# Two blocks on one core: the stores of a normalised memory, two small loads, and the order of the blocks in a mixer

## The chip, the cores and the metric

The kernel runs on one NeuronCore of a Trainium2 chip. Its engines run beside each other, each through its own list of instructions in order, and wait for one another by semaphores: PE (TensorE, matrix products), DVE (VectorE), ACT (ScalarE), POOL (GpSimd) and SP, which here only issues DMA transfers. The metric is device time in microseconds (us), the median of several runs.

## The reference, cut to what matters

The inputs are 512 tokens of width 1024 and a memory of 256 rows. Two transformer blocks run one after the other, in float32:

```
mod = c @ w_ada + b_ada                          # shift, scale, gate
h   = rmsnorm(x) * (1 + scale) + shift
y_a = (stick_breaking(q_a, k_a, v_a) * silu(z_a)) @ w_o_sb        # q_a.. = h @ w_in
y_b = (forgetting_attention(q_b, k_b, v_b, cumsum log f) * silu(z_b)) @ w_o_fox
x   = rmsnorm(x + gate * ((g0 * y_a + g1 * y_b) @ w_out), final_g)
# second block
h1  = rmsnorm(x);  q, k, v, u = h1 @ w_in_2
a   = rmsnorm((softmax(q1 k1) - lam * softmax(q2 k2)) @ v)        # 4 heads, q and k rotated
c   = silu(layernorm(causal_dwconv(u[:512] * sigmoid(u[512:]), 31 taps)))
x   = x + concat(a, c) @ w_out_2
x   = x + cross_attention(rmsnorm(x), rmsnorm(mem)) @ w_co        # needs mem @ w_ckv
x   = x + conv_ffn(rmsnorm(x));  out = rmsnorm(x)
```

`lam` comes from four vectors of 64 numbers (one load of 128 KB, each vector repeated on all partitions); the rotation's angles come from the positions (one load of 2 KB).

## The kernel before, in words

Every large product is done in three passes, so that float32 accuracy is kept: each operand is split into a rounded half `h` and a remainder `l`, and `wh*xh + wh*xl + wl*xh` are summed in PSUM (`mm3`). A weight unit is 128 x 1024 floats (512 KB). `load` (L153) brings one into one of three `wr` buffers, `split` makes `wh` on ACT (L166) and `wl` on DVE or POOL (L167); which of the two is given by letters, D or P, in strings such as `START_LO` and `B2_LO`. A `wr` buffer is free again when its `wl` is made.

**The front** is written out by hand (`manual_schedule`): there PE, ACT, DVE, POOL and SP each keep the order in which the program text names their instructions. It loads the memory (two tiles `mr`, split into the eight tiles `mt`), x (four loads `xt`), sixteen units of `w_ada` (`ada_load`, tag `ar`, eight buffers) and ten units of `w_ckv`. A loop over n = 0 to 9 does in each round: two `ada_load` (rounds 0 to 5), `mem_split(n + 2)` which also issues the load of unit n + 5, the squares of two of the eight parts of x (`squares_x`, rounds 0 to 3: ACT squares, DVE adds into `xacc`, L463), the products of unit n on PE (`mem_unit`), a few idle products (`spin`), and two `ada` steps (L447, a multiply and sum on DVE, then a small ACT step), two per round from round 1 to 8. In round 4 PE sums `xacc` (L517), the inverse root goes through DVE and ACT (L265 to L270), and in round 5 it is broadcast into `xrb`. From round 6 on `token_h` makes two parts of h a round: y on DVE (L469), the rounded half on ACT (L471), the remainder on DVE (L473). Everything after the front needs all eight parts of h.

**After the front** the eight tiles `mt` are stored to DRAM (`ms_d`, L536, 256 KB each); the mixer reads them back for the value products of the memory. This store loop stands outside the hand-written order, as do the loads of `lam` (L727, into a tile of the pool `smp`) and of the positions (L740, also `smp`) that stand in the text behind the heads of the first attention. What stands outside is placed by a planner at compile time: it takes each instruction when its inputs and buffers are free by its own estimate of times. It may put such instructions between those of the front on the same engine, and it does: the trace shows these DMAs, and the DVE and ACT work on `lam` and on the angles (L730 to L769), inside the front. A tile of a pool that is opened after the front's pools are closed lies on their memory, and has to wait until that is released.

**The mixer** is again written by hand for PE, ACT, DVE and POOL (SP's order is the planner's). `BLOCKS` lists 34 weight units in order: `q2`, `k2`, `v2` are projections by halves (two units for two heads), `u2:c` and `u2:c+4` make chunk c of the convolution's input, `cd:c` does taps 0 to 7 of chunk c as products with diagonal matrices on PE, `mv` are the memory's values, `wo2a` the output projection of the attention half. `AFTER` says which head step or norm step follows which block: q, k (transposes and splits), s (scores of the first row block), t (the other rows), x (transposes of the probabilities), v (values), n and o (norm of the head's output); l0 to l4 are the layernorm of the convolution (mean, squares, variance, broadcast, output). When `cd:c` is done, 15 taps are put into a list for DVE (L1075, each adds into the PSUM bank of the chunk), 8 into a list for ACT and POOL (L1069, L1070), and a last step adds the two (`ca`, L1081). After each block up to 4 of the first list and 3 of the second are emitted. Before a new `cd`, `fill(99)` emits all that is left of DVE's list, since all four chunks use the one bank `sm`.

## Time and profile before

| what | value |
|---|---|
| median of 3 runs (range) | 1298.86 us (1298.73 to 1303.45) |
| the profiled execution: its time, its span | 1301.26 us, 1299.5 us |
| PE busy | 1228.8 us, 95% of the span |
| weight loads of PE, DVE, ACT, POOL busy | 1031.6, 772.6, 604.3, 454.4 us |
| granted TensorE clock, mean | 0.977 |
| DMA over the span | 140.09 MB, mean 108 GB/s |

The page was taken on the one core. Busy times are sums of the instructions' own durations; a granted clock of 1.00 is 2.4 GHz, and a stretch at 0.65 was partly at 1.2 GHz. A time in brackets behind an instruction is how long its engine stood idle before it, and the arrow names what ended that. In the windows view the columns are the stretch, its length, then each engine's busy time with its count of instructions, the granted clock, the DMA share and the rate.

### The profile page before, as it was taken

To read this page: it belongs to the slowest core of one execution; us is meant where nothing else is said; L and a number is where in the kernel's file an instruction comes from. 1 tells how busy PE (TensorE), PEld (TensorE's weight loads), DVE (VectorE), ACT (ScalarE), POOL (GpSimd) and SP (SyncE) were. 2 spreads that over 40 slices of the span, in tenths; PEclk is the share of its full clock that TensorE was granted. 3 is DMA by queue.
4 is the path that set the end of the run, shared out by engine and by line. 5 is a ranking of instruction groups with operands and counts; after the bars stand their busy time and mean duration, and the time that the engine had idled before them with its cause. 6 is when DMAs were issued, how large, how long until landed. Compare 5 with 4: busy or idle time off the path is not lost.

```text
span 1299.5 us, 16841 instructions
## 1 busy us (share of the span) xinstructions
PE 1228.8 (95%) x6376; PEld 1031.6 (79%) x6381; DVE 772.6 (59%) x1241; ACT 604.3 (47%) x993; POOL 454.4 (35%) x303
## 2 busy tenths in 40 slices
PE   6699999999999999998898888999999999999997
PEld 4678887988878888886887776887888888888886
DVE  3775768555475274457577758466587777771113
ACT  3554566455663345356365535444444444442222
POOL 1464444322222138334572527203422222222321
PEclk9899999999999999999899888999999999999998
DMA  9734222232148342231143324211333332222221
GB/s 358 267 131 138 81 74 73 66 91 83 63 150 293 107 130 88 77 90 41 57 128 108 90 98 130 81 50 50 112 97 98 98 97 98 97 90 89 89 89 65
DMA packets 46017, 140.09 MB, mean 108 GB/s; under 512 B 5233, under 2 KB 8817, under 8 KB 45938
## 3 DMA queue, kind: packets, MB, share of 16 engines
q1 hardware_dynamic: 45170, 136.93, 32.6%
q0 software_dynamic: 768, 2.10, 0.4%
q8 instruction: 50, 0.82, 0.2%
q14 instruction: 29, 0.24, 0.1%
HBM read 127.48 MB, written 8.39 MB: 105 GB/s over the span
## 4 chain that ended last, share of the span: by engine, by line
PE 79%; DVE 10%; ACT 4%; DMA 3%; issue 2%; POOL 1%; SPq 0%; DVEq 0%; ACTq 0%; POOLq 0%
PE lin L148 66%; PE z L148 7%; PE pv L148 3%; PE sm L148 2%; DMA wr<-in_wts 2%; DMA ar<-in_wts 1%; PE z L612 1%; DVE ar L447 1%; DVE sm L1075 1%; DVE wl L167 1%; ACT wh L166 1%; DMA xt<-in_x_t 1%; POOL wl L167 1%; POOL rb L1070 0%; DVE h L225 0%
## 5 line engine op out<-in xcount | busy, mean ns | idle before, releaser
L148 PE MATMUL lin<-h,wh 128*128 128x512 f32 (+1 forms) x2232 | 693.6, 391 | 10.5 <-ACT wh L166 6.6
L148 PEld LDWEIGHTS lin<-h,wh 128*128 128x128 f32 x2232 | 416.8, 191 | 97.4 <-ACT wh L166 9.7
L148 PE MATMUL lin<-h,wl 128*128 128x512 f32 (+1 forms) x1116 | 432.6, 388 | 7.8 <-POOL wl L167 6.9
L167 POOL TENSOR_TENSOR wl<-wr,wh 128x1024 fp32r<-128x1024 f32 (+1 forms) x116 | 281.1, 2424 | 435.3 <-ACT wh L166 399.9
L166 ACT CAST wh<-wr 128x1024 fp32r<-128x1024 f32 (+1 forms) x197 | 204.5, 1040 | 253.0 <-PE lin L148 164.7
L148 PEld LDWEIGHTS lin<-h,wl 128*128 128x128 f32 x1116 | 213.0, 191 | 49.7 <-POOL wl L167 8.3
L167 DVE TENSOR_TENSOR wl<-wr,wh 128x1024 fp32r<-128x1024 f32 (+1 forms) x81 | 106.6, 1316 | 123.0 <-ACT wh L166 122.5
L148 PE MATMUL lin<-wh,h 128*128 128x256 f32 x672 | 127.4, 286 | 2.3 <-DVE h L1010 2.3
L148 PEld LDWEIGHTS lin<-wh,h 128*128 128x128 f32 x672 | 106.8, 193 | 2.8 <-issue 2.4
L1382 DVE SCALAR_TENSOR_TENSOR cv<-up,vecs,cv 128x512 f32<-128x512 f32 x88 | 94.2, 1071 | 18.3 <-ACT cv L1380 16.8
L148 PE MATMUL lin<-wl,h 128*128 128x256 f32 x336 | 95.7, 285 | 0.4 <-POOL wl L167 0.4
L148 PE MATMUL lin<-zz,wh 128*128 128x512 f32 (+1 forms) x324 | 91.5, 368 | 0.0
L683 POOL TENSOR_TENSOR zs<-zs,y 64x512 f32<-64x512 f32 x16 | 26.6, 1665 | 120.3 <-DVE y L682 104.2
L148 PEld LDWEIGHTS lin<-zz,wh 128*128 128x128 f32 x324 | 58.0, 187 | 11.6
L148 PEld LDWEIGHTS lin<-wl,h 128*128 128x128 f32 x336 | 64.7, 193 | 0.8 <-POOL wl L167 0.7
L148 PE MATMUL lin<-zz,wl 128*128 128x512 f32 (+1 forms) x162 | 59.6, 368 | 0.0
L321 POOL TENSOR_TENSOR nacc<-nacc,sq 128x512 f32<-128x512 f32 x34 | 52.6, 1558 | 16.7 <-ACT sq L320 16.2
L1377 POOL MEMSET up<- 128x2 f32 x44 | 4.3, 99 | 148.4 <-DVE cv L1382 116.3
L1075 DVE SCALAR_TENSOR_TENSOR sm<-cp,vecs,sm 128x512 f32<-128x512 f32 x60 | 45.2, 754 | 1.6
L218 DVE TENSOR_TENSOR tl<-z,th 128x512 fp32r<-128x512 f32 (+1 forms) x60 | 33.4, 595 | 17.1 <-ACT th L217 16.7
L1389 ACT ACTIVATE cv<-cv 128x512 f32<-128x512 f32 x22 | 13.9, 632 | 59.6 <-DVE cv L1382 59.6
L612 PE MATMUL z<-idf,p 128*128 128x128 f32 x200 | 34.3, 282 | 7.5 <-ACT p L1172 2.6
(398 smaller groups left out, 1717.8 us busy)
## 6 DMA issues: line engine op xcount, KB each, us to landing
wr<-in_wts SPq DMA_DIRECT2D x197, 512.0 KB, 3.5
ar<-in_wts SPq DMA_DIRECT2D x16, 512.0 KB, 6.8
qk<-qk SPq DMA_DIRECT2D x24, 128.0 KB, 2.2
wr<-in_wts SPq DMA_DIRECT2D x8, 384.0 KB, 3.0
xt<-in_x_t SPq DMA_DIRECT2D x4, 512.0 KB, 8.8
ms_d<-h SPq DMA_DIRECT2D x8, 256.0 KB, 7.9
kv_d<-kvo POOLq DMA_DIRECT2D x16, 128.0 KB, 4.2
ma_d<-gt SPq DMA_DIRECT2D x8, 256.0 KB, 5.3
```

The lines of the kernel that those rows point to most:

```text
L148: pe.matmul(o, lhsT=lhsT, rhs=rhs, start=start, stop=stop, skip_group_check=True)
L166: act.copy(out=hi[:, :n], in_=raw[:, :n])
L167: lo_engine().tensor_tensor(out=lo[:, :n], in0=raw[:, :n], in1=f32(hi[:, :n]), op=ALU.subtract)
L218: dve.tensor_tensor(out=lo, in0=src, in1=f32(hi), op=ALU.subtract)
L321: pool.tensor_tensor(out=acc, in0=acc, in1=q, op=ALU.add)
L447: dve.scalar_tensor_tensor(out=r, in0=r, scalar=1.0, in1=cb, op0=ALU.mult, op1=ALU.mult, accum_out=m)
L612: pe.transpose(z[:, o + i * P:o + (i + 1) * P], pt[rb_][:, ro:ro + P], ident)
L683: pool.tensor_tensor(out=zs[r], in0=zs[r], in1=y[r], op=ALU.mult)
L1075: dve.scalar_tensor_tensor(out=cz, in0=x_, scalar=w_, in1=cz, op0=ALU.mult, op1=ALU.add)
L1377: pool.memset(up[:, T:], 0.0)
L1382: dve.scalar_tensor_tensor(out=r, in0=up[:, 2 - j:2 - j + T], scalar=V("ffn_w", c * 3 + j), in1=r, op0=ALU.mult, op1=ALU.add)
L1389: act.activation(out=a, in_=a, func=AF.Silu)
```

## The change

- The store loop of `mt` is indented into the front's hand-written part, behind `memory_squares()`: SP issues the eight stores after all other DMAs of the front.
- `squares_x` comes before `mem_split(n + 2)` in each round.
- The remainder of the third unit of `w_ckv` is made on DVE (`START_LO`).
- The tiles of `lam` and of the positions move from `smp` to the pool `gp`, which is opened after the front is closed.
- In the mixer the blocks are reordered: `cd:1` stands 5 blocks after `cd:0` (before: 3), `cd:2` 7 after that (before: 5), `cd:3` 3 after that (before: 5); `q2`, `k2` of heads 2 and 3 come before `cd:1`; two `mv` units each stand between `cd:2` and `cd:3`, behind `cd:3` and between the `wo2a` units. The steps follow, and with them the letters of `B2_LO` and the place of `memory_back`.
- `cd:3` uses the PSUM bank `pv` instead of `sm`, and no `fill(99)` stands before it.

```diff
-START_LO = "DDPPPPPPPP"
+START_LO = "DDDPPPPPPP"
...
-B2_LO = 24 * "P" + 5 * "DP"
+B2_LO = 23 * "P" + "DPPDPDPDPDP"
...
-BLOCKS = ("q2:0 q2:1 k2:0 k2:1 u2:0 u2:4 v2:0 v2:1 u2:1 u2:5 cd:0 u2:2 u2:6 cd:1 q2:2 q2:3 k2:2 k2:3 cd:2 u2:3 u2:7 "
-          "v2:2 v2:3 cd:3 mv:2 mv:3 mv:4 mv:5 mv:6 mv:7 wo2a:0 wo2a:1 wo2a:2 wo2a:3")
+BLOCKS = ("q2:0 q2:1 k2:0 k2:1 u2:0 u2:4 v2:0 v2:1 u2:1 u2:5 cd:0 q2:2 q2:3 k2:2 k2:3 cd:1 u2:2 u2:6 v2:2 u2:3 u2:7 "
+          "v2:3 cd:2 mv:2 mv:3 cd:3 mv:4 mv:5 wo2a:0 wo2a:1 mv:6 mv:7 wo2a:2 wo2a:3")
 AFTER = {4: "q0", 5: "k0", 6: "s0", 7: "t0 q1", 8: "x0 k1", 9: "v0 s1", 10: "n0 t1", 11: "o0 x1", 12: "v1", 13: "n1",
-         14: "o1", 18: "q2", 19: "k2", 20: "s2", 21: "t2 q3", 22: "x2 k3", 23: "v2 s3", 24: "n2 t3", 25: "o2 x3",
-         26: "v3", 27: "n3", 28: "o3", 29: "l0 l1", 30: "l2", 31: "l3", 32: "l4"}
-BACK_AT = 23
+         14: "o1", 15: "q2", 16: "k2", 17: "s2", 18: "t2 q3", 19: "x2 k3", 20: "s3", 21: "t3", 22: "v2 x3", 23: "n2", 24: "o2 v3", 25: "n3", 26: "o3",
+         30: "l0 l1", 31: "l2", 32: "l3 l4"}
+BACK_AT = 22
...
-            mem_split(n + 2)
             for k in range(KD):
                 if SQ_AT[k] == n:
                     squares_x(k)
+            mem_split(n + 2)
             out_ = mem_unit(n)
...
         memory_squares()
-    for i, t in enumerate(mt):
-        nc.sync.dma_start(out=ms_d[i], in_=f32(t))
+        for i, t in enumerate(mt):
+            nc.sync.dma_start(out=ms_d[i], in_=f32(t))
...
-    lamt = smp.tile([P, T], F32, tag="sq", name="lamt")
+    lamt = gp.tile([P, T], F32, tag="f", bufs=3, name="lamt")
...
-    posi = smp.tile([P, NT], I32, tag="posi", bufs=1, name="posi")
+    posi = gp.tile([P, NT], I32, name="posi")
...
         if g == 0:
-            fill(99)
-            sums[c] = ps_sm()
+            if c < 3:
+                fill(99)
+            sums[c] = (ps_pv if c == 3 else ps_sm)()
```

## Rows read from the trace of the kernel before

**Rows 1.** Windows, whole kernel: stretch, length, busy time by engine, clock, DMA.
```profile
0.00:100.00 100.00, 78.13 (x437) 62.80 (x443) 61.73 (x109) 47.06 (x83) 41.79 (x32) 0.91 0.70 249
...
600.00:700.00 100.00, 85.36 (x534) 75.27 (x533) 72.74 (x147) 55.06 (x96) 57.09 (x37) 0.95 0.29 90
```

**Rows 2.** Waits of PE, whole kernel: who, for whom, total us, times, longest.
```profile
PE sm L148 <- DVE ca L1081: 9.5, 2, 8.6
...
PE xrb L517 <- DVE xacc L463: 5.7, 1, 5.7
```

**Rows 3.** Windows of 8 us in the front.
```profile
16.00:24.00 8.00, 6.07 (x47) 5.48 (x47) 1.90 (x1) 2.36 (x4) 3.01 (x2) 1.00 1.03 405
```

**Rows 4.** Timeline of SP in the front: start, duration, instruction, count.
```profile
7.58 4.79 SPq L442 DMA_DIRECT2D ar<-in_wts  x4
13.46 5.57 SPq L536 DMA_DIRECT2D ms_d<-h  x5
19.99 0.33 SPq L153 DMA_DIRECT2D wr<-in_wts  x1
...
57.95 1.47 SPq L442 DMA_DIRECT2D ar<-in_wts  x2
```

**Rows 5.** The page's DMA issues: count, size, median us to landing.
```profile
ms_d<-h SPq DMA_DIRECT2D x8, 256.0 KB, 7.9
```

**Rows 6.** Timeline of ACT in the front.
```profile
28.16 1.04 ACT L166 CAST wh<-wr 128x1024 fp32r<-128x1024 f32 x1 [8.41 <-DMA wr<-in_wts]
...
52.32 1.28 ACT L265 ACT_TABLE_LOAD   x1
...
53.84 1.28 ACT L766 ACT_TABLE_LOAD   x1
...
59.64 1.05 ACT L166 CAST wh<-wr 128x1024 fp32r<-128x1024 f32 x1
```

**Rows 7.** Timeline of DVE in the front.
```profile
37.45 2.42 DVE L463 TENSOR_TENSOR xacc<-xacc,xq 128x512 f32<-128x512 f32 x1 [1.12 <-ACT xq L462]
...
44.74 2.26 DVE L764 SCALAR_TENSOR_TENSOR ang<-rkh,ang 128x32 f32<-128x32 f32 x1
...
47.71 0.69 DVE L463 TENSOR_TENSOR xacc<-xacc,xq 128x512 f32<-128x512 f32 x1
...
56.70 1.21 DVE L447 SCALAR_TENSOR_TENSOR ar<-ar,cb 128x1024 f32<-128x1024 f32 x1
...
63.55 0.75 DVE L469 SCALAR_TENSOR_TENSOR y<-xt,gain,xrb 128x512 f32<-128x512 f32 x1
...
86.61 0.75 DVE L473 SCALAR_TENSOR_TENSOR h<-y,shift,h 128x512 fp32r<-128x512 f32 x1 [0.82 <-ACT h L471]
```

**Rows 8.** Windows in the mixer, all engines.
```profile
586.00:622.00 36.00, 24.89 (x131) 20.10 (x130) 26.02 (x58) 22.52 (x44) 19.70 (x14) 0.94 0.15 45
...
691.00:722.00 31.00, 23.28 (x134) 19.67 (x135) 22.88 (x56) 15.91 (x37) 7.50 (x6) 0.86 0.19 60
```

**Rows 9.** Windows with tile sm alone: products of cd:0, then cd:1 (no POOL column).
```profile
586.10:591.80 5.70, 5.70 (x24) 4.43 (x24) 0.00 (x0) 0.00 (x0) 1.00 0.00 0
621.90:630.50 8.60, 8.58 (x24) 6.49 (x24) 0.00 (x0) 0.00 (x0) 0.64 0.17 61
```

**Rows 10.** The page's groups: remainders on POOL and DVE, DVE's taps; count, busy, mean ns.
```profile
L167 POOL TENSOR_TENSOR wl<-wr,wh 128x1024 fp32r<-128x1024 f32 (+1 forms) x116 | 281.1, 2424 | 435.3 <-ACT wh L166 399.9
...
L167 DVE TENSOR_TENSOR wl<-wr,wh 128x1024 fp32r<-128x1024 f32 (+1 forms) x81 | 106.6, 1316 | 123.0 <-ACT wh L166 122.5
...
L1075 DVE SCALAR_TENSOR_TENSOR sm<-cp,vecs,sm 128x512 f32<-128x512 f32 x60 | 45.2, 754 | 1.6
```

**Rows 11.** Waits of PE, 655 to 800 us.
```profile
PE z L612 <- ACT p L1172: 2.6, 1, 2.6
...
PE pv L148 <- DVE kl0o L588: 2.1, 1, 2.1
PE z L1109 <- DVE nacc L1103: 1.3, 1, 1.3
```

## The prediction

> **What bounds the kernel now.** I read the windows of 100 us first: PE is full nearly everywhere, so time can only come from the stretches where it is not. Those are the first 100 us, with 78 of 100 busy, and the mixer from 600 us on, with 85 of 100 [rows 1]. The change touches just these two. The waits of PE, read next, name one large wait in each: the column sums of x wait 5.7 us for `xacc`, and the convolution's second chunk waits for the bank that `ca` of the first chunk frees, 8.6 of 9.5 us in two waits [rows 2].
>
> In the front the windows show the DMAs at their limit until about 40 us: 405 GB/s at a share of 1.03 [rows 3]. SP's timeline shows who uses that. Behind the first four `ar` loads, which end at 12.4 us, come five of the eight `ms_d` stores; they hold SP until 19.0 us, and the load of unit 3 of `w_ckv` is only issued at 19.99 [rows 4]. ACT then idles 8.4 us before the cast of that unit at 28.16 [rows 6]. Nobody needs those stores before the mixer. From there the front goes in rounds, each held together by ACT's order: the cast of unit 3 at 28.16, that of unit 7 at 59.64, four rounds on, thus 7.9 us a round [rows 6]. The last remainder of h ends at 86.61 + 0.75 = 87.4 us, and the dense work of PE starts with it [rows 7].
>
> **The change, part by part: the front.** *Stores last.* Eight stores of 256 KB are 2.1 MB, which at 405 GB/s is 5.2 us of a saturated DMA [rows 3, 5]. The load of unit 3 now follows the four `ar` loads directly: issued at about 13.5 in place of 20.0, 6.5 us earlier [rows 4]. Loads in this crowd took 8.2 us from issue to cast (19.99 to 28.16), and some of the crowd is still there, so I take 9.5 us: the cast comes at about 23, 5 us earlier.
>
> *Squares before the split, and the small work gone.* A round of the new front needs on ACT a cast of 1.04, two squares (half a cast's size, so about 0.6 each), two `ada` ends and a copy, together some 3.3 us; on DVE two adds of 0.69 and two `ada` of 1.2 each, 3.8 us if nothing is in the way [rows 6, 7]. In the old round DVE also did the angles, one of them 2.26 us long, and an add that took 2.42 instead of 0.69 [rows 7]; ACT put two table loads of 1.28 into the chain of the inverse root, one to bring the square root's table back after the exponential of `lam` and one for the sine [rows 6]. All of this leaves the front. The parts still wait for one another across the engines, so I don't take 3.8 but 5.2 us a round, an estimate: the old 7.9, less a share of those 2.6 us of tables, of the 2.26 and of the 1.7 of the slow add. Four rounds at 2.7 less are 10.7 us. `xacc` is then ready before PE has finished unit 4, and PE's 5.7 us of waiting with it. Sum so far 5 + 10.7 = 15.7 us.
>
> *Split of unit 2 on DVE.* A remainder takes 1.3 on DVE against 2.4 us on POOL [rows 10]: unit 2 is ready 1.1 us earlier and so is the load that takes its buffer. DVE is idle there (1.9 of 8 us busy between 16 and 24) [rows 3], so it costs nothing; I count it inside the 5 us. Without that cover it would cost 1.3.
>
> *What the stores now stand in front of.* SP issued the last two `ar` loads at 57.95 [rows 4]; 15 us earlier that is 43. The eight stores, their issue (1.1 us each in the crowd, 0.3 outside it) and their 5.2 us of transfer come behind them and ahead of the selector, the masks and the first weights of the attention. They are covered by the token part, 63.55 to 87.4 us before, where DVE, ACT and DVE take turns for each part of h [rows 7], and whose length I leave as it is. Left uncovered it is at most 5.2 us; I take 1.5, since ACT's order puts casts of those weights among the parts of h. The Trainium skill ("DMA: Bandwidth & Descriptors", Queues, rings and completion order) says that on each DMA engine descriptors are consumed in ring order. That speaks against the change here, as whatever is queued behind 2.1 MB starts after it; by it the whole 5.2 us would count, and the front's sum would be 10.5 in place of 14.2. The trace of before agrees on the direction: unit 3 behind five stores was late.
>
> *`lam` and positions later.* Their tiles lie on the front's memory, so their two DMAs start after the front. Some 25 short DVE instructions and a few of ACT with two or three table loads of 1.28 move to the heads of the first attention, where PE is full. Between 0 (idle slots) and 7.6 us (the work of both in a row: three tables 3.8 and the 2.26, with some small ones); I take 1. Should SP wait for the memory with weight loads queued behind that wait, PE would stand too; that is inside the 7.6.
>
> Front: 15.7 - 1.5 - 1 = 13.2 us gained; ends 5.2 - 7.6 = -2.4 (only the bytes saved, all work exposed) and 20 (of 22 us in which PE idles in the first 100).
>
> **The mixer.** *`cd:1` later.* Between `cd:0` and `cd:1` stood two units, now four (24 products of 512 columns are 5.7 us at full clock [rows 9]). That is 11 us more cover for the 15 taps of 0.75 [rows 10], against a wait of 8.6. The 9.5 us of waits for `ca` go [rows 2]; also what came with them: `cd:1` ran at a granted clock of 0.64, partly at 1.2 GHz, right after PE had stood still, and took 8.6 in place of 5.7, so 2.9 [rows 9]. Sum 12.4. What is late next: `n1` and `o1`, whose small DVE chain sits behind taps.
>
> *Heads 2 and 3 earlier and spread.* From 691 to 722 us PE idles 31 - 23.3 = 7.7 us, among it 2.6 for the probabilities of head 3 and 2.1 for the bank `pv` held by `k3` [rows 8, 11]. In the new order `cd:2` and `v2` stand between `t3` and `x3` (about 7.7 us of PE, before: one `mv` unit of 2.9 and `o2`), and three blocks between `k3` and `v2` in place of one. I take 6 of the 7.7 away, and 2 of the 3.3 us that the clock of 0.86 costs there (0.14 x 23.3).
>
> *What is added.* `cd:3` in `pv` follows `v3` directly and waits until ACT has squared and copied that bank: two passes of half a cast's size, 0.6 each, and the hand-over, 1.7 us; at worst 11 us, if ACT sits behind DVE's taps. The variance step `l2` now has one `mv` unit (24 products of 256 columns, half of 5.7) of cover in place of a `wo2a` unit; the wait of 1.3 [rows 11] becomes 1.3 + 2.9 = 4.2, so 2.9 more, and a slower clock after it, 1.5. DVE, 72% busy here [rows 1], has the same work in less time: the letters D in `B2_LO` are five before and after.
>
> Mixer: 12.4 + 8 - 1.7 - 2.9 - 1.5 = 14.3 us gained; ends 0 (each wait comes back as another) and 22 (nothing added).
>
> **Sum.** 13.2 + 14.3 = 27.5 us off the profiled execution's 1301.26. That one lies 2.4 above the median of the runs, 1298.86, and the difference is not part of it: 1271 us as a median.
>
> **The rivals.**
> (a) *The stall moves.* The mixer is bound by DVE and not by the bank: PE waits as long, only for softmax steps behind taps. For it: DVE was busy 26 of 36 us around the stall [rows 8]. Against: the other 10 of these 36 us it stood idle itself. Front alone: 1299 - 13 = 1286.
> (b) *The front keeps its rounds*, bound by the casts' and the DVE steps' turns; only the bytes are saved, less the 1 and the 1.5. For it: the rounds after 40 us ran at 7.9 us with the DMAs no longer full. Against: what filled them is taken out by name. 1299 - 2.7 - 14.3 = 1282.
> (c) *Both*: 1299 - 2.7 = 1296, no change that can be told; a measurement of this kernel tells 0.5%, 6.5 us, from none.
> (d) *Slower: the taps land on the heads.* No `fill` is forced before `cd:3`, and the taps of `cd:1` now fall on `s2`, `t2` and `x2`, those of `cd:2` and `cd:3` on `v2` to `o3`. If PE waits out 15 taps of 0.75, 11.3 us, for three chunks, and 4.6 us for `pv` and the variance, that is 38.5 added against 20.4 removed; with a front of 13.2 the kernel ends at 1299 + 18 - 13 = 1304. It decides from where the stretch between `cd:1` and `l0` takes longer than before. Against: at most four taps (3 us) go between two blocks of 3 to 9 us.
> (e) *The planner spoils it*: placed otherwise, the stores or small loads sit in SP's order ahead of weights. The stores are inside the written order, so this holds for the small loads alone, and is priced above.
>
> **Chances.** Forecast 0.66, (a) 0.14, (b) 0.11, (c) 0.05, (d) 0.04. The forecast's own range is 1258 (front 20, mixer 20) to 1280. The range to hold 8 of 10 reaches to (a) and (b): 1257 to 1287. Faster by over 0.5% 0.91, within 0.05, slower 0.04.
>
> **What would show it.** SP issues the eight stores behind the last `ar`; the cast of unit 3 comes near 23 us and that of unit 7 near 44; no table load of the sine before the last part of h, which ends near 73. In the mixer no wait of `cd:1` for `ca`, its 24 products in 5.7 us at full clock, PE busy over 90% from 586 us (less the shift) on, a new wait of `cd:3` for ACT's copy of `pv`, and a wait of 4 us before the variance. Wrong would be: rounds still near 8 us, or the 8.6 us found again under another name.

## The result and the profile after

The changed kernel takes 1287.2 us (median of 4 runs, 1285.3 to 1287.8), beside 1298.8 us for the kernel before on the same chip; the ratio of the means is 0.9902, with a 95% interval from 0.9875 to 0.9928. It is faster by 11.6 us where 27.5 were forecast, and its profiled execution has a span of 1286.0 us in place of 1299.5.

Two windows of the changed kernel answer to [rows 1]. In the first 100 us PE is busy 83.1 in place of 78.1 us, in the hundred from 600 on 89.5 in place of 85.4: both stalls shrank, and neither is gone.

```profile
0.00:100.00 100.00, 83.09 (x510) 70.99 (x511) 68.42 (x120) 49.62 (x90) 41.44 (x32) 0.90 0.74 264
600.00:700.00 100.00, 89.51 (x565) 78.98 (x563) 75.94 (x166) 60.31 (x117) 53.30 (x35) 0.95 0.32 101
```

I set the two traces side by side at five marks, each the start of one kind of instruction on PE. Differences are before less after, so that what is gained grows from mark to mark.

| mark (first start on PE) | before, us | after, us | difference |
|---|---|---|---|
| product into `z` for `va`, the attention's dense start | 88.45 | 80.36 | 8.1 |
| column sums that open the mixer | 520.85 | 513.44 | 7.4 |
| `cd:0` | 586.10 | 580.17 | 5.9 |
| column sums of the cross-attention | 812.95 | 800.37 | 12.6 |
| end of the span | 1299.5 | 1286.0 | 13.5 |

So the front gave 8.1 us where 13.2 were forecast, and the mixer, from its column sums to those of the cross-attention, 5.2 (292.1 to 286.9) where 14.3 were. From `cd:0` on it gave 6.7; the 1.5 before that were lost to the clock, as the section on the experiments shows.

**The front after.** The timelines of ACT and DVE answer to [rows 6, 7]. The cast of unit 3 comes at 24.30 in place of 28.16 and that of unit 7 at 46.52 in place of 59.64; the first part of h starts at 50.43 in place of 63.55, and its last remainder ends at 70.86 + 0.75 = 71.6 in place of 87.4. That is 15.8 us earlier, and forecast were 15.7. But only 13.1 of them were there at the first part of h; the other 2.7 were gained among its parts, a stretch that the prediction left as it was. Before, ACT stood idle there for two of the attention's weights (third fence below, from the kernel before); afterwards it waits for none among the parts of h, which would account for it.

```profile
24.30 1.04 ACT L166 CAST wh<-wr 128x1024 fp32r<-128x1024 f32 x1 [4.45 <-DMA wr<-in_wts]
46.52 1.05 ACT L166 CAST wh<-wr 128x1024 fp32r<-128x1024 f32 x1
...
63.06 0.69 ACT L471 ACTIVATE h<-y,shift 128x512 fp32r<-128x512 f32 x1 [0.34 <-DVE y L469]
63.65 1.03 ACT L166 CAST wh<-wr 128x1024 fp32r<-128x1024 f32 x1
...
66.47 1.06 ACT L166 CAST wh<-wr 128x1024 fp32r<-128x1024 f32 x1
```

```profile
50.43 0.75 DVE L469 SCALAR_TENSOR_TENSOR y<-xt,gain,xrb 128x512 f32<-128x512 f32 x1
...
70.86 0.75 DVE L473 SCALAR_TENSOR_TENSOR h<-y,shift,h 128x512 fp32r<-128x512 f32 x1 [0.81 <-ACT h L471]
```

```profile
74.62 1.05 ACT L166 CAST wh<-wr 128x1024 fp32r<-128x1024 f32 x1 [2.60 <-DMA wr<-in_wts]
...
77.54 1.05 ACT L166 CAST wh<-wr 128x1024 fp32r<-128x1024 f32 x1 [1.10 <-DMA wr<-in_wts]
```

Yet PE's dense work starts only 8.1 us earlier. SP's timeline says why: the eight stores hold SP from 46.35 to 53.14, the masks and the selector follow, and the first weight of the attention is issued at 54.91; ACT casts it at 63.65 (above). PE's timeline shows the price, a wait of 3.40 us for that cast and one of 2.11 for the next. Before, the products with these two weights ran among the parts of h, from 74.10 to 88.45; now most of them stand behind those parts, up to 80.36. And behind the two waits PE ran at half its clock: the window from 67.58 to 72.38 shows PE busy all the time at a granted clock of 0.51, which is the lower of its two levels, 1.2 GHz, nearly throughout. Before, the clock was 1.00 through this stretch.

```profile
46.35 6.79 SPq L536 DMA_DIRECT2D ms_d<-h  x8
...
54.91 16.01 SPq L153 DMA_DIRECT2D wr<-in_wts  x4
```

```profile
64.74 0.73 PE L148 MATMUL lin<-h,wh 128*128 128x512 f32 x2 [3.40 <-ACT wh L166]
67.58 1.22 PE L148 MATMUL lin<-h,wh 128*128 128x512 f32 x2 [2.11 <-ACT wh L166]
...
80.36 0.40 PE L148 MATMUL z<-wh,h 128*128 128x256 f32 x2
```

```profile
67.58:72.38 4.80, 4.80 (x11) 3.84 (x12) 2.36 (x4) 2.93 (x4) 2.98 (x3) 0.51 0.66 178
```

**The mixer after.** The window of the products of `cd:1` (tile `sm` alone) answers to [rows 9]: 5.86 us at a granted clock of 1.00, where it took 8.60 at 0.64.

```profile
619.84:625.70 5.86, 5.83 (x24) 4.40 (x24) 0.00 (x0) 0.00 (x0) 1.00 0.30 89
```

Over the stretch from `cd:0` to the cross-attention's column sums, the window of the kernel before (first) and that of the changed one (second) show what became of it. PE was idle 226.85 - 196.41 = 30.4 us and is idle 220.20 - 193.56 = 26.6; its work became 2.9 us shorter, with the clock at 0.95 in place of 0.92.

```profile
586.10:812.95 226.85, 196.41 (x1094) 167.34 (x1093) 160.34 (x307) 118.71 (x207) 113.99 (x70) 0.92 0.29 92
```

```profile
580.17:800.37 220.20, 193.56 (x1097) 165.14 (x1097) 162.67 (x307) 119.22 (x208) 114.33 (x71) 0.95 0.30 95
```

PE's waits in that stretch of the changed kernel (total us, times, longest) answer to [rows 2, 11]. The 9.5 us for `ca`, the 2.6 for `p` and the 2.1 for `kl0o` are gone. In their place stand `ah`, `cp`, remainders on POOL and DVE, and two waits of the norm for `nacc`.

```profile
PE pv L148 <- ACT ah L1198: 4.1, 1, 4.1
PE z L1110 <- DVE nacc L1104: 3.9, 1, 3.9
PE lin L148 <- ACT wh L166: 3.3, 1, 3.3
PE z L148 <- DVE wl L167: 2.8, 1, 2.8
PE lin L148 <- DVE cp L1023: 2.7, 1, 2.7
PE lin L148 <- POOL wl L167: 2.5, 2, 2.4
PE z L1095 <- DVE nacc L1085: 2.1, 1, 2.1
PE lin L148 <- ACT bch L297: 1.8, 1, 1.8
PE lin L148 <- DVE wl L167: 1.2, 1, 1.2
```

### The profile page after: what moved, and what is told of

The parts are those of the page before. It is cut to its first block, busy times and chain, and to the rows that moved or that the text cites. A ratio compares the mean times of both kernels' runs of the same rounds, so it can differ in the third digit from the quotient of the medians.

```text
span 1286.0 us, 16873 instructions
## 1 busy us (share of the span) xinstructions
PE 1225.6 (95%) x6381; PEld 1031.9 (80%) x6381; DVE 779.6 (61%) x1242; ACT 599.4 (47%) x989; POOL 451.6 (35%) x302
## 5 line engine op out<-in xcount | busy, mean ns | idle before, releaser
L167 POOL TENSOR_TENSOR wl<-wr,wh 128x1024 fp32r<-128x1024 f32 (+1 forms) x115 | 277.7, 2416 | 473.6 <-ACT wh L166 449.7
L167 DVE TENSOR_TENSOR wl<-wr,wh 128x1024 fp32r<-128x1024 f32 (+1 forms) x82 | 111.6, 1361 | 127.8 <-ACT wh L166 127.4
L321 POOL TENSOR_TENSOR nacc<-nacc,sq 128x512 f32<-128x512 f32 x34 | 53.0, 1568 | 14.9 <-ACT sq L320 14.3
L697 DVE TENSOR_TENSOR_SCAN om<-om 128x511 f32<-128x511 f32 (+3 forms) x32 | 35.9, 1162 | 9.5 <-ACT om L693 9.4
L1379 DVE TENSOR_TENSOR up<-lin,rb 128x512 f32<-128x512 f32 x44 | 30.1, 686 | 16.1 <-PE lin L148 13.4
```

The costliest lines, as they stand in the source:

```text
L167: lo_engine().tensor_tensor(out=lo[:, :n], in0=raw[:, :n], in1=f32(hi[:, :n]), op=ALU.subtract)
L321: pool.tensor_tensor(out=acc, in0=acc, in1=q, op=ALU.add)
L697: dve.tensor_tensor_scan(out=om[:, o:e], data0=om[:, o:e], data1=om[:, o:e], initial=1.0, op0=ALU.mult, op1=ALU.bypass)
L1379: dve.tensor_tensor(out=up[:, :T], in0=o, in1=rb[:, 0], op=ALU.mult)
```

## The experiments

Ratios are to the kernel before, run beside each (1299.7 to 1301.9 us), with their intervals. Executions of one program spread over some 3 us and more, part of it before the mixer (last section), so edits of the mixer are also read from the stage's own length in the profile: 286.9 us in the changed kernel, and 286.4 to 287.4 in four other executions with the same mixer (e2, e3, e5, e12), but 290.7 in a fifth (e16).

Windows of these profiles show that this spread is the clock's. From the column sums to `cd:0` the instructions and PE's waits (2.9 to 3.0 us) are the same, and the stretch takes 65.3 us at a granted clock of 1.00 (before, e2, e4, e12 and others) or 66.8 at 0.97 (changed kernel, e3, e5, e16 and others). From `cd:0` on the six executions with the changed mixer leave PE idle for 26.6 to 27.4 us; what differs is PE's busy time, 193.2 to 194.2 us at 0.94 to 0.95 and, in e16, 196.7 at 0.92. So the length can hide or feign some 4 us, and PE's idle time from `cd:0` on is the safer measure of an edit. Each number is from one execution.

| kernel | from `cd:0` on, us | PE idle, us | granted clock |
|---|---|---|---|
| before | 226.9 | 30.4 | 0.92 |
| changed mixer, six executions | 220.2 to 223.9 | 26.6 to 27.4 | 0.92 to 0.95 |
| e4 | 220.7 | 24.8 | 0.93 |
| e7 | 221.1 | 25.8 | 0.94 |
| e8 | 223.4 | 26.9 | 0.93 |
| e9 | 234.8 | 38.7 | 0.91 |
| e10 | 236.5 | 37.5 | 0.91 |
| e13 | 220.8 | 24.2 | 0.93 |
| e14 | 217.1 | 24.1 | 0.93 |
| e17 | 224.1 | 27.1 | 0.93 |
| e6 | 217.4 | 22.7 | 0.94 |
| e15 | 218.3 | 23.3 | 0.93 |
| e18 | 212.3 | 19.8 | 0.95 |

**e1 and e2: each half of the change alone.** e1 (first) takes the mixer's order, letters and banks back, e2 (second) the front's edits.

```
-B2_LO = 23 * "P" + "DPPDPDPDPDP"
+B2_LO = 24 * "P" + 5 * "DP"
...
-            sums[c] = (ps_pv if c == 3 else ps_sm)()
+            sums[c] = ps_sm()
```

```
-START_LO = "DDDPPPPPPP"
+START_LO = "DDPPPPPPPP"
...
-        for i, t in enumerate(mt):
-            nc.sync.dma_start(out=ms_d[i], in_=f32(t))
+    for i, t in enumerate(mt):
+        nc.sync.dma_start(out=ms_d[i], in_=f32(t))
```

> The front's edits alone; the mixer's order, its letters and banks are those of before. The prediction valued this part at 13.2 us gained. Theory now (the first weights of the attention stand behind the 2.1 MB of stores, which eats half of the front's gain): about 7.5 us gained, some 1291 us; the last part of h ends near 72 us and PE waits some 5 us for the first weights between 60 and 70 us. Rival (the front gained its 13 and the rest was lost in the mixer by a clock or an order that the front upsets): 1286 or less.

> The mixer's edits alone; front as before. The prediction valued this part at 14.3 us gained. Theory now (the first half gains 11.8 us, the second loses 6.5 us to a wait of cd:3 for ACT's copy, remainders of weights behind taps on DVE and the norm's two waits): about 5.5 us gained, some 1293 us, with the same waits as in the changed kernel: 4 us for pv at cd:3 and about 4 us before the variance. Rival (the mixer's losses came from the front's moved work, the shifted clock or DMA phase): 10 us gained or more, 1289 or less.

e1: 1293.6 us, ratio 0.9938 [0.9918, 0.9959], 8.1 us gained. e2: 1294.3 us, 0.9946 [0.9932, 0.9961], 7.0 us gained. In their profiles `va` starts at 79.93 (e1), and the mixer takes 286.8 (e2). The halves add, within their intervals, to what the changed kernel gains; each has its own loss, and no upset of one by the other is seen.

**e3: the stores among the rounds.**

```
+            for i, t in enumerate(mt):
+                if 4 + i // 2 == n:
+                    nc.sync.dma_start(out=ms_d[i], in_=f32(t))
```

> The changed kernel, with its eight stores issued two at a time after units 4 to 7 of the front, ahead of its last loads, in place of all eight behind the last one. Theory (stores ahead of the first attention weights): the loads of those weights are issued some 5 to 6 us earlier, PE's waits for ACT's cast and the remainder at 61 to 67 us (3.4 + 2.1 us) go, the kernel gains 4 to 6 us, about 1282. Rival 1 (ACT's order holds the casts back, not the loads): within 1.5 us of the changed kernel. Rival 2 (the stores slow the rounds wherever they stand): the last part of h ends 2 us or more later than 72 us, and the gain is under 2 us or negative.

1287.8 us, 0.9896 [0.9879, 0.9914]: nothing gained. It did not move what it meant to: `ar` loads that wait for their buffer stand ahead of the stores on SP, so six of the eight were still issued from 46.6 to 51.7 us and the first weight at 54.25. It left the question open.

**e5: the stores behind the first two weights.**

```
+    with tc.issue_after(<SP's load of the first ka unit>):
+        for i, t in enumerate(mt):
+            nc.sync.dma_start(out=ms_d[i], in_=f32(t))
```

> The changed kernel, with the eight stores issued on SP behind the loads of the first two weights of the attention instead of ahead of the masks and the selector. The run that spread the stores over rounds left six of them at 46.6 us, ahead of those weights, and gained next to nothing, so the question is still open. Theory (the first weights wait for 2.1 MB ahead of them): their loads are issued near 48 us in place of 54.9 and cast before 60 in place of 63.7; PE's waits of 3.4 and 2.1 us at 61 to 67 us go, and the first product of va comes 4 to 6 us before 80.4 us; about 4 to 6 us gained on the changed kernel. Rival 1 (the written order of ACT and DVE, with a part of h every 2.4 us, holds the casts): va not more than 1.5 us earlier. Rival 2 (the stores then delay the third and fourth weight): va's start is early, and PE waits as long for the weights of va.

1279.8 us, 0.9823 [0.9804, 0.9842]. SP's, ACT's and PE's timelines of this kernel: the two weights are issued from 53.12 us on, the stores start at 58.11, the casts come at 57.80 and 62.02, and `va` starts at 73.67, 6.7 us earlier than in the changed kernel.

```profile
53.12 4.95 SPq L155 DMA_DIRECT2D wr<-in_wts  x2
58.11 5.83 SPq L708 DMA_DIRECT2D ms_d<-h  x8
```

```profile
57.80 1.04 ACT L168 CAST wh<-wr 128x1024 fp32r<-128x1024 f32 x1
...
62.02 1.05 ACT L168 CAST wh<-wr 128x1024 fp32r<-128x1024 f32 x1 [1.08 <-DMA wr<-in_wts]
```

```profile
73.67 0.40 PE L148 MATMUL z<-wh,h 128*128 128x256 f32 x2
```

The theory holds: the place of the stores is what cost. With 88.45 - 73.67 = 14.8 us the front now gives what its terms promised without the stores' cost. Both rivals fall as they were stated, but the first has a part in it. The first weight was issued 1.8 us earlier, landed 4.1 us after its issue in place of 6.7 (from the views of tile `wr`), and was cast 0.6 us after landing in place of 2.0: together 5.9. So the transfer behind the stores is 2.6 of it, and 1.4 is ACT's order, in which this cast stands behind the third part of h here and behind the fifth in the changed kernel. For the second weight the order is the larger part: issued at the same time, landed 1.3 us earlier, cast 4.5 earlier. Both casts stand outside the hand-written order; that the planner put them later because it, too, reckoned with the stores fits, but is not shown.

At `va` the 6.7 us are 3.7 of a later start of the first product (61.08 here), 0.9 of a longer wait for the second weight, and some 2.1 left for the slow clock; 4.80 us at 0.51 are 2.4 more than at full clock, an estimate. In e5 the clock is 1.00 through this stretch.

The Trainium skill ("DMA: Bandwidth & Descriptors", Queues, rings and completion order) has descriptors consumed in ring order on each engine. This pair of runs agrees, with 6.7 and 4.1 us from issue to landing.

**e12 and e16: what shortened the rounds.** e12 puts the tiles of `lam` and the positions back into memory that is free early; e16 puts the squares behind the split and unit 2's remainder on POOL, as before.

```
-    lamt = gp.tile([P, T], F32, tag="f", bufs=3, name="lamt")
+    lamt = smp.tile([P, T], F32, tag="sq", name="lamt")
...
-    posi = gp.tile([P, NT], I32, name="posi")
+    posi = smp.tile([P, NT], I32, tag="posi", bufs=1, name="posi")
```

```
-START_LO = "DDDPPPPPPP"
+START_LO = "DDPPPPPPPP"
...
+            mem_split(n + 2)
             for k in range(KD):
                 if SQ_AT[k] == n:
                     squares_x(k)
-            mem_split(n + 2)
```

> The changed kernel with lam's and the positions' tiles back in memory that is free from the start, so that their loads, the angle work and the table loads may go back among the front's rounds. It splits the term of 10.7 us that the prediction gave to shorter rounds. Theory (a good part of it was this small work): the first part of h starts 3 to 8 us later than at 50.4. Rival (squares ahead of the split and the earlier loads did it alone): under 1 us later.

> The changed kernel with the squares of x behind the split again and unit 2's remainder back on POOL. It splits the front's gain up to the first part of h (13.1 us: from 63.55 to 50.43), of which the small work was 1.5. Theory (the stores and the squares share the rest, with the rounds as the larger part, as predicted): the first part of h comes 4 us or more later than 50.4. Rival (the stores' bytes did nearly all, and the rounds shorten by themselves once the loads are early): under 2 us later.

In e12 the first part of h starts at 51.92 us, 1.5 later than in the changed kernel (1285.7 us in all, 0.9877 [0.9854, 0.9900]). In e16, by the timelines of ACT and DVE, rounds take 7.68 us again and the first part of h starts at 58.07, 7.6 later (1291.9 us, 0.9931 [0.9908, 0.9954]).

```profile
31.40 1.04 ACT L166 CAST wh<-wr 128x1024 fp32r<-128x1024 f32 x1
...
39.08 1.04 ACT L166 CAST wh<-wr 128x1024 fp32r<-128x1024 f32 x1
```

```profile
58.07 0.75 DVE L469 SCALAR_TENSOR_TENSOR y<-xt,gain,xrb 128x512 f32<-128x512 f32 x1
```

Of the 13.1 us by which that part came earlier, 7.6 belong to e16's two edits, 1.5 to the small work, and the other 4.0 are left for the stores, which fits unit 3's cast coming 3.9 us earlier; that last part was not run by itself. And although h was 7.6 us later in e16, `va` started only 1.7 later, at 82.08: in the changed kernel PE did not wait for h, but for weights and then ran at half its clock, while e16 kept 1.00 there.

**e4: `cd:3` one unit later.**

```
-          "v2:3 cd:2 mv:2 mv:3 cd:3 mv:4 mv:5 wo2a:0 wo2a:1 mv:6 mv:7 wo2a:2 wo2a:3")
+          "v2:3 cd:2 mv:2 mv:3 mv:4 cd:3 mv:5 wo2a:0 wo2a:1 mv:6 mv:7 wo2a:2 wo2a:3")
```

> The changed kernel, with the chunk cd:3 and the unit mv:4 exchanged in the written order, so that one unit lies between the head's last product into pv and the chunk that takes this bank. Theory (the wait is for ACT's copy of pv alone): the wait of 4.05 us shrinks to under 1.5 and the chunk runs in 5.7 in place of 7.4 us; 4 to 5 us gained, about 1282.5. Rival (DVE is the bound there, with taps and remainders behind one another): the wait comes back at the next bank, h or the norm, and the gain is under 1.5 us.

1283.4 us, 0.9871 [0.9852, 0.9890], but 4.2 us of its lead lie ahead of the mixer, where its instructions are those of the changed kernel. The mixer took 286.0 us, 0.9 less, but from `cd:0` on 220.7, 0.5 more: what it gained lies ahead of the edit. PE's idle time fell by 1.8 us and its busy time grew by 2.3 at a lower clock. The wait for `ah` is gone, and the one before the mean grew from 2.1 to 6.2 us:

```profile
PE z L1095 <- DVE nacc L1085: 6.2, 1, 6.2
```

The taps of `cd:3` now come a block later and the mean waits for them. The rival had the size right for the time; of the idle time slightly more went.

**e7: a longer cover for the variance.** 

```
-          "v2:3 cd:2 mv:2 mv:3 cd:3 mv:4 mv:5 wo2a:0 wo2a:1 mv:6 mv:7 wo2a:2 wo2a:3")
+          "v2:3 cd:2 mv:2 mv:3 cd:3 mv:4 mv:5 wo2a:0 wo2a:1 mv:6 wo2a:2 mv:7 wo2a:3")
```

> The changed kernel with mv:7 and wo2a:2 exchanged alone, so that the variance step has a unit of 5.8 us of cover and the step behind it one of 2.9. Theory (the cover was too short, as the prediction's own step had it): the wait of 3.9 us before the variance falls under 1, the unit after it runs at full clock, up to 1.5 us of new waiting before the broadcast; 2 to 4 us gained. Rival (DVE is late there, not PE early): the same wait comes back in front of the broadcast, under 1 us gained.

1285.8 us, 0.9880 [0.9862, 0.9897]. The wait before the variance fell from 3.9 to 1.3, 0.7 came back before the broadcast, and the stage took 287.9 us: not shorter, with PE idle 25.8 us, 0.8 under the spread. The expected 2 to 4 us are not shown.

**e8 and e9: taps left out.** e8's edit; e9 has `c < 1` in its place.

```
-        fill_v.extend(lambda j=j: vector_tap(j) for j in range(8 * CV_UNITS[c], 31 - npool))
+        fill_v.extend(lambda j=j: vector_tap(j) for j in range(8 * CV_UNITS[c], 31 - npool) if c < 3)
```

> The changed kernel without the fifteen taps of the last chunk on DVE; that part of the convolution is left out, so 15 times 0.75 = 11.3 us of DVE's work are gone. Theory (in the second half PE waits for an order on ACT and PE's early arrival, with DVE only in part the bound): the wait of 4.05 us at cd:3 and that of 3.9 before the variance stay, those before the mean (2.1) and for remainders behind taps (1.2, 2.4) go; 3 to 5 us gained. Rival (DVE's taps are the bound of the whole second half): nearly all of the 19 us of waits between 655 and 770 us go, 9 us gained or more. Rival 2 (taps don't matter): under 1.5 us.

> The changed kernel without the fifteen DVE taps of chunks 1, 2 and 3 (left out of the convolution; chunk 0 keeps its own): 34 us of DVE's work gone from the mixer. Theory (the new waits of the second half, 2.7 us for cp, 4.1 for pv, 1.2 for a remainder on DVE, come from DVE's queue, where softmax steps, taps and remainders stand behind one another): these three fall to under 1 us each, what comes back is waits for casts and remainders of weights; the stretch from cd:0 to the cross-attention (220.2 us) shortens by 4 to 8 us. Rival (the written order and the weights' own pace hold PE, taps or not, as the run without the last chunk's taps suggests): the stretch shortens by under 2 us.

e8: 1291.1 us, 0.9922 [0.9907, 0.9937], the mixer 290.1. e9: 1301.3 us, 1.0003 [0.9991, 1.0015], the mixer 300.1. Neither gained what was expected. e8's idle time (26.9 us) is that of the changed mixer, its extra length a lower clock; e9 went the other way, with 12 us more of idle time. The edit does more than it says. The end of a chunk (`last`) is queued behind its DVE taps and first flushes all that is left of the eight taps on ACT and POOL. With no DVE taps it comes at once, and ACT's timeline of e9 shows those taps in one row, each waiting for POOL as the one below, with the cast behind them at 695.99:

```profile
691.30 0.73 ACT L1070 ACTIVATE cpr<-cp,vecs 128x512 f32<-128x512 f32 x1 [0.66 <-POOL rb L1071]
```

They can't tell whether DVE is the bound.

**e13: the taps made thin.** The order is kept.

```
-            dve.scalar_tensor_tensor(out=cz, in0=x_, scalar=w_, in1=cz, op0=ALU.mult, op1=ALU.add)
+            n = 16 if c else T
+            dve.scalar_tensor_tensor(out=cz[:, :n], in0=x_[:, :n], scalar=w_, in1=cz[:, :n], op0=ALU.mult, op1=ALU.add)
```

> The changed kernel with the forty-five DVE taps of chunks 1 to 3 cut to 16 of their 512 columns (the rest of these taps is left out): the written order and every pacing stay as they are, some 25 us of DVE's work go. It repairs the two runs that dropped taps altogether: there the eight taps of ACT and POOL, no longer paced, came in one block, and the mixer grew longer by up to 13 us. Theory (in the second half PE waits behind DVE's queue): the waits for cp (2.7), pv (4.1), a DVE remainder (1.2) and the mean (2.1) shrink by half or more; from cd:0 to the cross-attention the stretch takes 208 to 215 us in place of 220. Rival (the written order and the weights' pace, not DVE): over 218 us, the same waits.

1286.1 us, 0.9884 [0.9865, 0.9903]; the stretch from `cd:0` took 220.8 us, not shorter than 220.2. DVE worked 143.6 us in it in place of 162.7. PE's idle time fell by 2.4 us, most of it the 2.1 before the mean, and a lower clock (0.93) took that back. PE's waits:

```profile
PE pv L148 <- ACT ah L1199: 4.4, 1, 4.4
PE z L1111 <- DVE nacc L1105: 3.9, 1, 3.9
...
PE lin L148 <- DVE cp L1023: 3.3, 1, 3.3
```

So the time of DVE's taps is not the bound: 19 us less of it took 2.4 us of idle time, where 5 to 12 us were expected. The rival holds. The timelines of ACT and DVE show what `cd:3` waits for:

```profile
691.00 0.72 ACT L1070 ACTIVATE cpr<-cp,vecs 128x512 f32<-128x512 f32 x1 [1.31 <-POOL rb L1071]
691.63 1.03 ACT L166 CAST wh<-wr 128x1024 fp32r<-128x1024 f32 x1
...
695.41 0.69 ACT L224 ACTIVATE h<-lin,sg 128x512 fp32r<-128x512 f32 x1 [2.26 <-DVE lin L1215]
...
696.47 0.59 ACT L1199 COPY ah<-pv 128x512 f32<-128x512 f32 x1
```

```profile
692.70 2.07 DVE L167 TENSOR_TENSOR wl<-wr,wh 128x1024 fp32r<-128x1024 f32 x1 [1.97 <-ACT wh L166]
694.69 0.68 DVE L1215 TENSOR_TENSOR lin<-ah,lin 128x512 f32<-128x512 f32 x1
```

A tap on ACT waits for POOL; a cast stands behind it; the cast's remainder on DVE, 2.07 us, stands ahead of head 2's output; that output's copy on ACT stands ahead of the copy of head 3's bank; and for this one `cd:3` waits. No engine is full there: the written order makes one chain of three queues. The changed kernel's timelines show the same chain, with its cast at 694.39 and the copy of head 3's bank at 699.22.

**e10 and e11: `cd:1` alone later.** The old order, steps and banks of the mixer, with `cd:1` two units later and `cd:2` one (the diff is to the order of before); e11 has e5's stores besides.

```
-BLOCKS = ("... cd:0 u2:2 u2:6 cd:1 q2:2 q2:3 k2:2 k2:3 cd:2 u2:3 u2:7 v2:2 v2:3 cd:3 mv:2 ..."
+BLOCKS = ("... cd:0 u2:2 u2:6 q2:2 q2:3 cd:1 k2:2 k2:3 u2:3 cd:2 u2:7 v2:2 v2:3 cd:3 mv:2 ..."
```

> The changed kernel with the mixer's order of before in its second half: heads 2 and 3 at their old places, cd:3 in its old bank with its fill, the norm covered by units of wo2a; only cd:1 comes two units later (and cd:2 one), so that its wait for the bank is covered. Theory (moving cd:1 is what gains in the mixer, and the rest of the new order loses what its heads gain): the mixer, from its column sums to those of the cross-attention, takes 280 to 284 us (before 292.1, changed kernel 286.9), 3 to 6 us gained on the changed kernel. Rival (the heads' new places gain as forecast, and the losses belong to cd:1's move): 289 us or more, slower than the changed kernel by 2 us or more.

> The changed kernel with both mended: the stores behind the first two weights of the attention, and in the mixer cd:1's move alone. Theory: the two gains add, 6.5 us in the front and 3 to 6 in the mixer; 1274 to 1278 us, below both kernels. Rival (an earlier front takes cover from the mixer, the gains don't add): 1280 or more.

e10: 1300.1 us, 0.9998 [0.9982, 1.0014], the mixer 301.7. The mixer took 17.7 us more than the upper end of what was expected, and for a plain reason: only three units now lay between `cd:1` and `cd:2`, and the bank wait came back there with 12.2 us. At `cd:1` itself four units, two of them `u2`, left 6.0.

```profile
PE sm L148 <- DVE ca L1081: 18.2, 2, 12.2
```

e11: 1294.0 us, 0.9948 [0.9928, 0.9969], the mixer 300.0. Both kernels lose in the mixer, but e11 is 6.5 us below e10: the stores' mend of e5 holds its worth beside another mixer.

**e14: heads 2 and 3 at their old places.** The first half as changed, the chunks at least four units apart, the norm covered as before, `cd:3` in its old bank.

```
-BLOCKS = ("... k2:2 k2:3 cd:1 u2:2 u2:6 v2:2 u2:3 u2:7 v2:3 cd:2 mv:2 mv:3 cd:3 mv:4 mv:5 wo2a:0 ..."
+BLOCKS = ("... k2:2 k2:3 cd:1 u2:2 u2:6 u2:3 u2:7 cd:2 v2:2 v2:3 mv:2 mv:3 cd:3 mv:4 mv:5 mv:6 mv:7 wo2a:0 ..."
-... 15: "q2", 16: "k2", 17: "s2", 18: "t2 q3", 19: "x2 k3", 20: "s3", 21: "t3", 22: "v2 x3", 23: "n2", ...
+... 18: "q2", 19: "k2", 20: "s2", 21: "t2 q3", 22: "x2 k3", 23: "v2 s3", 24: "n2 t3", 25: "o2 x3", 26: "v3", ...
```

> The changed kernel with its first half of the mixer as it is (cd:1 four units behind cd:0), but the steps of heads 2 and 3 where they stood before, among cd:2 to mv:6, cd:3 in its old bank and the norm covered by units of wo2a. It isolates the step 'heads 2 and 3 earlier and spread', which the prediction valued at 8 us less 6.1 for what is added. Theory (the spreading gains the waits of the heads, and its new waits give most of that back): the mixer takes 285 to 290 us, within 3 us of the changed kernel's 286.9. Rival 1 (the new places lose net): under 284. Rival 2 (without the spread the bank wait returns at cd:2 or cd:3, as it did with 12.2 us where only cd:1 was moved): 291 or more.

1283.9 us, 0.9868 [0.9849, 0.9887], the mixer 283.9 us. That is 8.2 us less than before, and 3.0 less than with the spread heads, though it has large waits of its own, for the bank held by the k step and before the mean:

```profile
PE pv L148 <- DVE kl0o L588: 6.8, 1, 6.8
PE z L1094 <- DVE nacc L1084: 6.8, 1, 6.8
```

By the profile the first rival holds: the spread, with what it adds, lost 3 us, 2.5 of it idle time, outside the spread of the changed mixer. The interval of its ratio overlaps that of the changed kernel, so the sign is likely and the size is not sure.

**e17: `v2:2` behind `u2:3` and `u2:7`.** `v2:2` opens two of the three `lin` banks and holds them until `v2:3`; the change put both `u2` units between.

```
-... cd:1 u2:2 u2:6 v2:2 u2:3 u2:7 "
+... cd:1 u2:2 u2:6 u2:3 u2:7 v2:2 "
           "v2:3 cd:2 ...
```

> The changed kernel with v2:2 behind u2:3 and u2:7 instead of ahead of them. In the changed order v2:2 opens two of the three banks named lin and holds them over both u2 units until v2:3, so that these share the one that is left: u2:7 waited 2.7 us for cp, the copy of u2:3's bank, and then ran 7.35 in place of 5.7 us. Cutting the taps on DVE left this wait at 3.3 us. Theory (the banks): the wait for cp at u2:7 goes, the unit takes 5.7 us; 3 to 4.5 us gained in the mixer. Rival (DVE comes as late wherever the units stand): the wait comes back at the next place where DVE is waited for, the head's k step or v2's results; under 1 us.

1287.0 us, 0.9899 [0.9886, 0.9913]. The wait for `cp` is gone, so the banks made it, not DVE's taps. But the rival's size holds: a wait for the copies of the k step came in its place, that for `ah` grew, and PE's idle time stayed at 27.1 us. The stage took 289.4 us; the 2.5 us more are a lower clock (0.93), not waits.

```profile
PE pv L148 <- ACT ah L1198: 5.0, 1, 5.0
PE z L148 <- DMA qk<-qk: 2.6, 1, 2.6
```

**e6, e15 and e18: mends together.** e6 has e4's and e7's exchanges, two remainders moved from DVE to POOL and six taps a block behind `cd:3` (the diff shows these last two); e15 is e6 with e5's stores; e18 is e15 with e17's order.

```
-B2_LO = 23 * "P" + "DPPDPDPDPDP"
+B2_LO = 23 * "P" + "DPPDPPPDPPP"
...
-            fill(FILL_V)
+            fill(6 if cds == 4 else FILL_V)
```

> The changed kernel with four edits in the second half of the mixer: cd:3 and mv:4 exchanged, mv:7 and wo2a:2 exchanged (the variance is covered by a unit of 5.8 us), the remainders of two units moved from DVE to POOL, and six taps in place of four after each block once cd:3 is through. Theory (the end of the mixer is set by the taps of cd:3, queued on DVE in a written order that leaves gaps, and by the norm's cover): the wait before the mean, 6.2 us with cd:3 exchanged alone, falls under 3, that before the variance, 3.0 to 3.9, under 1.5; 4 to 7 us gained on the changed kernel between the column sums that open the mixer and those of the cross-attention (404.2 us there). Rival (DVE is full, whatever the order): under 1.5 us.

> The changed kernel with the stores behind the first two weights of the attention and with the four edits in the second half of the mixer that took 2.7 us off that stage. Theory: va starts at 73.7 in place of 80.4 and the mixer takes about 284.3; some 9 us gained on the changed kernel, 1276 to 1280. Rival (the gains don't add, since the earlier front changes nothing there but the mixer's edits lose elsewhere): not faster than the kernel with the stores behind alone, 1280.

> The changed kernel with all mends: the stores behind the first two weights, the four edits in the second half of the mixer, and v2:2 behind the u2 units. Theory: 3 us less than the same kernel without the last (1276.8), about 1274; the mixer 280 to 281 us in place of 283.6. Rival (the mixer's other waits take it up): 1276 or more.

e6: 1286.2 us, 0.9894 [0.9875, 0.9913], the mixer 284.2: 2.7 us off the stage where 4 to 7 were expected, and too little to tell in the total. e15: 1276.8 us, 0.9823 [0.9803, 0.9842], the mixer 283.6; the same ratio as e5, so the four edits are not shown to add anything. e18: 1271.5 us, 0.9780 [0.9759, 0.9800], the mixer 278.9. Its window from `cd:0` on shows PE idle 212.28 - 192.48 = 19.8 us in place of 26.6.

```profile
571.48:783.76 212.28, 192.48 (x1097) 165.18 (x1097) 157.43 (x305) 119.05 (x208) 120.16 (x73) 0.95 0.32 99
```

The exchange that gained nothing by itself (e17) is worth 4.6 us of the stage where the waits behind it are mended too, 3.5 of it idle time; the intervals of e15 and e18 just part. e18 beats both kernels: 28.6 us below the one before by the ratio (0.022 x 1299.7), some 16 below the changed one.

## Why the prediction was wrong

- **Stores last, rounds, xacc.** Right in kind, and in sum by luck: 15.8 us measured at the last part of h, 15.7 forecast. The bytes gave about 4 (5 forecast), the shorter rounds 9.1 (10.7); the 2.7 that fill the sum up came among the parts of h, where I had expected nothing. Of the 9.1, 7.6 come from the squares ahead of the split and unit 2's remainder, and only 1.5 from the small work, to which I had given tables, a slow angle and a slow add. I misread those two: the slowness did not leave with the small work. In the changed front a DVE operation of 128x4 takes 2.14 us, and it ends with a remainder on POOL (below, DVE and POOL), as the slow angle did before (44.74 + 2.26 = 47.0, beside a remainder on POOL from 44.62 to 46.95). The wait for `xacc` fell from 5.7 to 0.3.

```profile
40.51 2.14 DVE L267 TENSOR_TENSOR rq<-xrc 128x4 f32<-128x4 f32 x1
```

```profile
40.25 2.37 POOL L167 TENSOR_TENSOR wl<-wr,wh 128x1024 fp32r<-128x1024 f32 x1 [0.18 <-ACT wh L166]
```

- **What the stores now stand in front of: this step failed.** I took 1.5, with 5.2 as the upper end; e5 measures 6.7 at `va`. I reasoned that the parts of h cover the first weights, since ACT's order puts their casts among these parts; but h itself became 15.8 us earlier, so the weights had to be as much earlier to stay under it. Their first cast came only 6.7 us earlier (70.38 to 63.65). The stores in front of them, and the later places of the casts in ACT's order, held them. The cost also lies above my end of 5.2, because I priced the transfer alone: of the 6.7, some 2.1 are the slow clock behind PE's two waits, for which I had no term.
- **`lam` and positions later.** Taken at 1, and not to be told apart: from `va` to the mixer the changed kernel took 433.1 us, the one before 432.4 and e12, which undoes the step, 430.5, all within that stage's own spread.
- **`cd:1` later.** Right: the 9.5 us of waits and the slow clock behind them went, `cd:1` in 5.86 us at full clock. e10 shows the condition I had not named: every pair of chunks needs its distance. The count of units is not enough either: four units, two of them `u2`, left a wait of 6.0 there, and four of `q2` and `k2` left none in the changed kernel; that `u2` leaves DVE less time for the taps is likely and not shown.
- **Heads 2 and 3 spread, and what is added: this step failed.** The waits named there did go (`p` and `kl0o`, and most of `th` and `smc`). The added ones were priced at 4.6 us (1.7 for `pv`, 2.9 for the variance). By the lists of waits before and after, 21.4 us of waits went (9.5 of them for `ca`) and 17.5 came: the variance as said (2.6 more), `ah` with 4.1 in place of 1.7, and 10.8 I had not seen: 2.7 for `cp` because `v2` holds two of three banks (e17), 2.1 before the mean, 3.7 for remainders behind other work, the rest for casts, remainders and small ones around the norm and behind it. I looked at each step's own cover and not at what its instructions stand behind on ACT and POOL (e13).
- **Rivals.** (a), the stall moves to softmax steps behind taps, gave 1286, the time that came, but not by its mechanism: the front too fell short, and e13 leaves the taps 2.4 us. (b), and (c) with it, is excluded by the rounds, (d) by the stretch from `cd:0` on, which became shorter. (e) named the danger, stores ahead of weights, and dismissed it as belonging to the planner: it was in the written order itself.

What stays open: why the granted clock differs between executions with the same waits (0.97 and 1.00 before `cd:0`, 0.92 to 0.95 behind it), and how the 3 us of e14 split between heads, norm and banks.

## What to carry to other kernels

When a stage gets shorter, price each transfer that was moved behind it against the new start of what comes next, not the old one: the cover shrinks with the stage. A stall in an order written out by hand is a chain over several in-order queues; a fix of one link showed nothing here (e7, e17) and the links together did (e18), so follow the chain through every engine, and count the banks each open accumulation holds, before pricing a step. To test whether an engine is the bound, make its work smaller in place (e13), rather than leave it out (e8, e9), which changes the pacing of everything queued behind it. And compare idle time beside length: a change of the clock can look like 4 us of an edit.

## What the runs showed of the hardware

Small DVE work is far dearer beside POOL. The four angle products (128x8 each) took 0.62 us together in the front of the kernel before, with no remainder on POOL at that time; moved into the first attention they took 5.59, while POOL made two remainders, as the timelines of DVE and POOL in the changed kernel show.

```profile
81.88 5.59 DVE L749 TENSOR_SCALAR ang<-idf,posf 128x8 f32<-128x8 f32 x4
```

```profile
82.43 4.74 POOL L167 TENSOR_TENSOR wl<-wr,wh 128x1024 fp32r<-128x1024 f32 x2
```

The Trainium skill ("SBUF — State Buffer", Who interferes with whom) has DVE and GpSimd share a pair of ports by an exclusive lock, the one that comes second blocked for a whole instruction. The trace agrees in size: 4.74 us for POOL's two remainders, and the DVE operations end 0.3 us behind them.

The stretch between `va` and the mixer's column sums, which no edit but that of the small loads touches, took from 429.6 to 433.6 us in different executions. Part of it is one wait of PE for a remainder on POOL near 390 us: 1.8 us in the changed kernel, 0.5 in e4, none in the kernel before. An edit of one stage can be masked by such a difference in another, so stages are best compared by their own length.
